# Attention of a hybrid decoder layer: units of four heads of a key group instead of two

## The chip, the cores and the metric

The kernel runs on one core of a Trainium2 chip. The core has five engines with an instruction queue each: TensorE (PE) for matrix products, VectorE (DVE), ScalarE (ACT), GpSimd (POOL) and SyncE (SP), which here only issues transfers. Matrix products land in PSUM, eight banks of 512 float32 columns on 128 partitions; everything else works from SBUF. An engine works its queue in order. The metric is the device time of one execution in microseconds (us).

## What is computed

One layer of a decoder on 1024 tokens of width 1024, all in float32. After a normalization and one input projection, eight attention heads (two key groups of four heads, head width 64) and eight groups of a gated spatial mixer run side by side; their outputs are joined, projected, normalized and added; then comes a SwiGLU feed-forward part. The change touches the attention alone. Every head has three branches, mixed by gates:

```python
o_c = softmax(q kc + bias) vc          # 63 compressed blocks
o_s = softmax(q ks + bias) vs          # selected blocks: all 16 are selected, so plain causal attention
o_w = softmax(q kw + bias) vw          # sliding window of 512 tokens
o = gb[..., 0:1] * o_c + gb[..., 1:2] * o_s + gb[..., 2:3] * o_w   # gb = sigmoid(gate logits)
```

The four heads of a group share their keys and values.

## The kernel before

Precision is kept by splitting each operand into a high part, rounded to the format that PE reads fast, and a low part, the rest. `split` (L165) makes both: the high part by a copy (ACT, L167), the low part by a subtraction (DVE, L173). `mm3` (L182) multiplies two split operands by three matmuls.

The attention loop (L640) goes over eight tiles of 128 query tokens, from tile 7, with most keys, to tile 0. In a tile it goes over the two key groups and over two pairs of heads in each: a unit is (tile, group, pair), 32 in all. A unit does the following.

- `load_q` (L568), two units ahead: two transfers from the scratch tensor `q_scr` on SP's queue into `qr`, and a split by POOL into `qt` (three buffers).
- For each head: logits by two matmuls for each chunk of columns (L674, L675) into one of two banks `ps_a`; DVE adds the position bias and keeps a running minimum (`biased`, L679; `plain`, L683) and writes them to a probability buffer `L`, one for each head, out of a ring of six; ACT takes the exponential of the three branches and their sums (L722).
- Three small instructions on DVE make the weights of the branches, gate divided by sum (L725 to L728), and POOL scales the probabilities by them (L733).
- Value products: a block is 128 keys. For two blocks PE transposes the scaled probabilities of both heads (L745) into a bank `ps_t` of 512 columns, out of three; `split` makes `ph` and `pl`; then each block takes two matmuls of 256 columns (L752, L754), which add up in the one bank `ps_p` over all blocks of the unit. The values hold high and low parts in 64 columns each, so that ACT copies the lower half of the result (`otmp`, L756) and DVE adds it to the upper half (`os`, L759); a last split makes `mixh` and `mixl`.

`output_proj` of the tile before (48 matmuls in the banks `ps_w`, two loads on POOL's queue, `xt` and the store of `h1` on SP's) stands ahead of the second of the four units of a tile, `pre_ffn` (eight transposes, two stores) ahead of the fourth. `with tc.high_priority(n)` moves what stands in it ahead by a number of places; a planner fixes each engine's order of instructions from that before the run, and the chip only waits on semaphores.

In SBUF, pools are laid on two stacks, and a pool that takes the place of an earlier one waits for the last user of it. On the left stack the attention's pools lie over the transposed input, first `pt`, `mix` and `late`, then `L` (its six pools taken from the top down), `o` and `q`. The feed-forward stage, written over the same room, starts when they come free. The value and gate projections `v_proj` (L482) run just ahead of the attention, tokens 4 to 7 of the input in the order 4, 5, 6, 7 and then 0 to 3, their banks taken in turn from `ps_w`, `ps_p` and `ps_t`.

## Time and profile before

| what | value |
|---|---|
| median of three runs | 1249.96 us (1245.37 to 1250.56) |
| profiled execution | 1250.03 us |
| its span, first to last instruction | 1248.3 us |
| mean granted clock of PE over the span | 0.993 of full speed |
| attention on DVE, first logit scan to last output split | 247.9 to about 595 us |

The profile is that of one execution. Busy time of an engine counts the time in which at least one of its instructions is under way; matmuls overlap each other in it, since the next starts while the one before still drains. PEld is the loading of weights into PE. A line such as L745 is one of the kernel's file; operations of a helper carry the helper's line.

### The profile page before, as it was taken

What the parts mean: (1) busy time and instruction counts of PE and PEld (TensorE: products, weight loads), DVE (VectorE), ACT (ScalarE), POOL (GpSimd) and SP (SyncE); (2) the same over time, 40 slices, a digit from 0 to 9 for tenths busy, and PEclk for the clock granted to TensorE, in tenths of its full rate; (3) what the DMA queues carried; (4) which work ended last, traced back from release to release, by engine and by line L of the source; (5) the groups of instructions that cost most, each with busy time, mean ns of one, the idle gap of its engine ahead of it and who ended that gap; (6) DMA issues with size and microseconds to landing.
All of it is one profiled execution on the core that took longest, in us unless ns stands there. A gap on an engine that the chain in (4) does not pass through costs nothing.

```text
span 1248.3 us, 18189 instructions
## 1 busy us (share of the span) xinstructions
PE 1201.0 (96%) x6074; PEld 1008.8 (81%) x6074; DVE 922.4 (74%) x2071; ACT 568.4 (46%) x1254; POOL 383.4 (31%) x454
## 2 busy tenths in 40 slices
PE   6999999889999999998899999999999999999997
PEld 5888878878888888887687888888888888888886
DVE  5646237668898988986599887876787647588996
ACT  4423022246777878886544332333332324444452
POOL 3315113155445446562051222201222101132341
PEclk9999999999999999999999999999999999999999
DMA  7212453321021121424414233223233189332235
GB/s 259 86 66 87 135 178 117 106 93 48 10 81 43 48 81 48 140 77 137 145 65 152 100 120 127 94 89 108 91 127 124 53 287 359 122 110 85 94 119 202
DMA packets 106229, 143.86 MB, mean 115 GB/s; under 512 B 8120, under 2 KB 64792, under 8 KB 106136
## 3 DMA queue, kind: packets, MB, share of 16 engines
q1 hardware_dynamic: 99552, 133.43, 32.4%
q0 software_dynamic: 2304, 4.20, 1.2%
q10 hardware_dynamic: 4280, 5.08, 1.2%
q8 instruction: 48, 0.79, 0.3%
q14 instruction: 45, 0.37, 0.1%
HBM read 103.60 MB, written 40.71 MB: 116 GB/s over the span
## 4 chain that ended last, share of the span: by engine, by line
PE 84%; DVE 9%; ACT 2%; issue 2%; DMA 1%; POOL 1%; SPq 0%; DVEq 0%; POOLq 0%; ACTq 0%
PE fb L185 16%; PE fb L183 15%; PE fb L184 15%; PE ps_w L183 4%; PE ps_w L184 4%; PE ps_w L185 4%; PE ps_a L183 4%; PE ps_a L184 3%; PE ps_a L185 3%; PE ps_t L745 3%; PE ps_p L754 2%; PE ps_p L752 2%; PE ps_a L674 2%; PE ps_a L675 2%; DVE pl L173 1%
## 5 line engine op out<-in xcount | busy, mean ns | idle before, releaser
L967 DVE TENSOR_TENSOR cc<-fb,cc 128x512 f32<-128x512 f32 x140 | 94.2, 685 | 55.9 <-PE fb L185 55.1
L722 ACT ACTIVATE L<-L,mm 128x64 f32<-128x64 f32 (+8 forms) x192 | 116.2, 608 | 37.0 <-DVE mm L679 36.2
L733 POOL TENSOR_SCALAR L<-L,wts 128x64 f32<-128x64 f32 (+8 forms) x192 | 108.4, 588 | 74.1 <-DVE wts L728 53.4
L848 POOL TENSOR_TENSOR cc<-sil 128x512 f32<-128x512 f32 x22 | 35.2, 1601 | 287.4 <-issue 226.3
L173 DVE TENSOR_TENSOR pl<-ps_t,ph 128x512 fp32r<-128x512 f32 (+1 forms) x160 | 101.6, 643 | 11.2 <-ACT ph L167 10.6
L167 ACT CAST op<-s 128x512 fp32r<-128x512 f32 x80 | 49.4, 620 | 121.5 <-PE fb L185 106.7
L184 PE MATMUL fb<-wdo,hido 128*128 128x512 f32 x264 | 102.7, 389 | 0.0
L183 PE MATMUL fb<-wdo,hido 128*128 128x512 f32 x264 | 101.9, 389 | 0.0
L185 PE MATMUL fb<-wdo,hido 128*128 128x512 f32 x264 | 100.4, 389 | 0.0
L184 PE MATMUL fb<-b_b,op 128*128 128x512 f32 x256 | 99.6, 389 | 0.0
L183 PE MATMUL fb<-b_b,op 128*128 128x512 f32 x256 | 99.3, 389 | 0.0
L185 PE MATMUL fb<-b_b,op 128*128 128x512 f32 x256 | 99.3, 389 | 0.0
L167 ACT CAST ph<-ps_t 128x512 fp32r<-128x512 f32 (+1 forms) x160 | 84.4, 555 | 25.6 <-PE ps_t L745 23.1
L745 PE MATMUL ps_t<-ident,L 128*128 128x128 f32 x592 | 88.6, 274 | 1.5 <-DVE pl L173 0.9
L674 PE MATMUL ps_a<-kt,qt 128*128 128x448 f32 (+4 forms) x208 | 74.7, 363 | 7.3 <-DVE L L683 2.8
L173 DVE TENSOR_TENSOR hido<-hidr,hido 128x512 fp32r<-128x512 f32 x77 | 60.8, 801 | 27.3 <-ACT hido L167 27.2
L167 ACT CAST hido<-hidr 128x512 fp32r<-128x512 f32 x77 | 47.4, 619 | 66.3 <-PE fb L185 22.8
L1046 POOL TENSOR_TENSOR tt<-wdr 128x512 f32<-128x512 f32 x22 | 36.1, 1644 | 134.5 <-DVE wdo L173 80.1
L754 PE MATMUL ps_p<-pl,vt 128*128 128x256 f32 x264 | 74.3, 303 | 3.1 <-DVE pl L173 3.0
L745 PEld LDWEIGHTS ps_t<-ident,L 128*128 128x128 f32 x592 | 68.9, 141 | 9.5 <-POOL L L733 1.8
L167 ACT CAST op<-wraw 128x512 fp32r<-128x512 f32 x60 | 37.1, 622 | 84.3 <-PE fb L185 75.6
L173 DVE TENSOR_TENSOR op<-s,op 128x512 fp32r<-128x512 f32 x80 | 63.9, 804 | 14.6 <-ACT op L167 13.8
(359 smaller groups left out, 3468.2 us busy)
## 6 DMA issues: line engine op xcount, KB each, us to landing
wraw<-in_w_gate_up_dram SPq DMA_DIRECT2D x40, 512.0 KB, 3.6
hidr<-hid_scr SPq DMA_DIRECT2D x77, 256.0 KB, 2.7
hid_scr<-sil SPq DMA_DIRECT2D x44, 256.0 KB, 2.0
wdr<-in_w_down_dram SPq DMA_DIRECT2D x44, 256.0 KB, 5.5
hid_scr<-cc SPq DMA_DIRECT2D x33, 256.0 KB, 2.0
xt<-in_x_dram SPq DMA_DIRECT2D x16, 512.0 KB, 3.6
raw<-in_w_in_dram SPq DMA_DIRECT2D x16, 512.0 KB, 4.3
gm_scr<-gmt SPq DMA_DIRECT2D x16, 256.0 KB, 2.6
```

The source lines that it names most:

```text
L167: nc.scalar.copy(hi, src)
L173: e.tensor_tensor(lo, src, fl(hi), op=ALU.subtract)
L183: nc.tensor.matmul(ps, sh, mh, start=first, stop=False)
L184: nc.tensor.matmul(ps, sh, ml, start=False, stop=False)
L185: nc.tensor.matmul(ps, sl, mh, start=False, stop=last)
L674: nc.tensor.matmul(ps[:, :w], qt[:, 0, hh, :], kt_[g][:, c0:c0 + w], start=True, stop=False)
L722: nc.scalar.activation(L[:, c0:c1], L[:, c0:c1], AF.Exp, bias=mm[:, col:col + 1], scale=-1.0, accum_out=sums[:, hh, br:br + 1])
L733: nc.gpsimd.tensor_scalar(pts[hh][:, c0:c1], pts[hh][:, c0:c1], wts[:, hh, br:br + 1], 1.0, op0=ALU.mult, op1=ALU.mult)
L745: nc.tensor.transpose(ps[:, (bi * 2 + hh) * P:(bi * 2 + hh + 1) * P], pts[hh][:, c0:c0 + P], ident)
L754: nc.tensor.matmul(pv[:, :256], v, pl[:, bi * 256:(bi + 1) * 256], start=False, stop=last)
L967: nc.vector.tensor_tensor(dst, ps, y_, op=ALU.add)
L1046: eng.tensor_tensor(dst, x_, y_, op=op)
```

## The change

A unit becomes (tile, group, first head, number of heads): four heads at once, two units for a tile, except that group 0 of the first tile stays in two units of two heads. That makes 17 units instead of 32.

- A group of value products is one block of four heads, and each product has 512 columns. One `ph` and `pl` hold one block instead of two.
- The ring `L` has eight buffers instead of six and lies last on the stack, above `o` and `q`. In tiles 2 to 0 two heads share a buffer and only the first four pools of the ring are used (`l_tile`).
- `load_q` loads four heads, one unit ahead, with one `qr` and two `qt` buffers.
- `gates` keeps 1 + exp(-x), without the reciprocal; the weights are 1 / (max(sum, 1e-30) * gates), by one combined instruction and one reciprocal.
- `output_proj` of the tile before stands ahead of the tile's last unit, `pre_ffn` between that unit's scaling and its value products. The priority numbers differ.
- `otmp` and `os` hold four heads, so that two sums of 64 x 256 and one split of 128 x 256 end a unit.

```diff
@@ gate
         nc.vector.tensor_scalar(gv_, gv_, 1.0, None, op0=ALU.add)
-        nc.vector.reciprocal(gv_, gv_)
@@ pools
-    for nm in ("pt", "mix", "late", "L", "o", "q"):
+    for nm in ("pt", "mix", "late", "o", "q", "L"):
         if nm == "L":
-            at[nm] = Ring("at_L", 6, "left")
-            at[nm].pools.reverse()
+            at[nm] = Ring("at_L", 8, "left")
...
+    def load_q(i, g, r0, nr):
+        qr = at["q"].tile([P, R, P], F32, name="qr", bufs=1)
+        h0 = g * R + r0
         for dup in range(2):
+            nc.sync.dma_start(out=qr[64 * dup:64 * dup + 64, :nr],
+                              in_=q_scr[h0:h0 + nr, :, i * P:(i + 1) * P].rearrange("h d t -> d h t"))
+        qt = at["q"].tile([P, 2, R, P], F32R, name="qt", bufs=2)
+        split(qt[:, 0, :nr], qt[:, 1, :nr], qr[:, :nr], "pool", "pool")
         return qt
...
-    order = [(i, g, pr) for i in TILES for g in range(G) for pr in range(2)]
+    order = [(7, 0, 0, 2), (7, 0, 2, 2), (7, 1, 0, 4)]
+    order += [(i, g, 0, 4) for i in TILES[1:] for g in range(G)]
+    QAHEAD = 1
...
+    packed = {}
+
+    def l_tile(i, n):
+        w = 64 + P * (i + 1) + P * min(i + 1, 5)
+        if i >= 3:
+            return at["L"].tile([P, 64 + S + 640], F32, "L")
+        if n % 2 == 0:
+            turn_ = packed["turn"] = packed.get("turn", -1) + 1
+            packed["t"] = at["L"].pools[turn_ % 4][1].tile([P, 64 + S + 640], F32, name="L")
+            return packed["t"][:, :w]
+        return packed["t"][:, 864:864 + w]
...
-    HP0, HP, HP2, HO, HF, HQ, HS, HV = 400, 100, 150, 100, 400, 300, 600, 200
+    HP0, HP, HP2, HO, HF, HQ, HS, HV = 400, 200, 250, 150, 500, 500, 900, 300
...
+        for un, unit in enumerate(units_):
+            _, g, r0, nr = unit
+            lastu = un == len(units_) - 1
+            if lastu and ti > 0:
+                with tc.high_priority(HO):
+                    pend = output_proj(TILES[ti - 1])
...
-                wts = small.tile([P, 2, 3], F32, name="wts")
-                nc.vector.tensor_scalar(wts, sums, 1e-30, None, op0=ALU.max)
-                nc.vector.reciprocal(wts, wts)
-                nc.vector.tensor_tensor(wts, wts, gates[...], op=ALU.mult)
+            nc.vector.scalar_tensor_tensor(wts[:, :nr], sums[:, :nr], 1e-30, gates[...], op0=ALU.max, op1=ALU.mult)
+            nc.vector.reciprocal(wts[:, :nr], wts[:, :nr])
...
+            if lastu and ti > 0:
+                with tc.high_priority(HF):
+                    pre_ffn(TILES[ti - 1], *pend)
             with tc.high_priority(HV):
...
-                    groups = [blocks[b:b + 2] for b in range(0, len(blocks), 2)]
+                n_ = nr * P
+                per = 512 // n_
+                groups = [blocks[b:b + per] for b in range(0, len(blocks), per)]
...
-                            nc.tensor.matmul(pv[:, :256], v, ph[:, bi * 256:(bi + 1) * 256], ...)
-                            nc.tensor.matmul(pv[:, :256], v, pl[:, bi * 256:(bi + 1) * 256], ...)
+                        nc.tensor.matmul(pv[:, :n_], v, ph[:, bi * n_:(bi + 1) * n_], ...)
+                        nc.tensor.matmul(pv[:, :n_], v, pl[:, bi * n_:(bi + 1) * n_], ...)
...
-                    tmp = at["o"].tile([64, 256], F32, name="otmp", bufs=OB)
+                tmp = at["o"].tile([64, 512], F32, name="otmp", bufs=OB)
```

## Rows read from the trace of the kernel before

**Rows 1.** The page's first part: busy us of each engine, share, instructions.
```profile
PE 1201.0 (96%) x6074; PEld 1008.8 (81%) x6074; DVE 922.4 (74%) x2071; ACT 568.4 (46%) x1254; POOL 383.4 (31%) x454
```

**Rows 2.** Windows: stretch and length, then busy us (instructions) by engine, granted clock.
```profile
core 0: us, PE busy (x) PEld busy (x) DVE busy (x) ACT busy (x) POOL busy (x), PEclk, DMA share, GB/s
250.00:300.00 50.00, 44.69 (x270) 38.82 (x270) 35.80 (x133) 27.92 (x64) 28.25 (x33) 0.93 0.27 85
300.00:550.00 250.00, 241.64 (x1584) 212.13 (x1583) 218.60 (x866) 194.29 (x520) 123.46 (x214) 1.00 0.21 64
550.00:600.00 50.00, 42.55 (x236) 35.43 (x235) 37.69 (x128) 35.34 (x106) 16.08 (x38) 0.96 0.47 148
```

**Rows 3.** PE's timeline (start, duration), a window of the feed-forward stage, one transpose.
```profile
359.99 0.28 PE L754 MATMUL ps_p<-pl,vt 128*128 128x256 f32 x1
...
360.34 0.28 PE L752 MATMUL ps_p<-ph,vt 128*128 128x256 f32 x1
360.46 0.60 PE L745 MATMUL ps_t<-ident,L 128*128 128x128 f32 x4
...
750.00:800.00 50.00, 50.00 (x222) 41.41 (x221) 37.34 (x54) 15.01 (x25) 6.50 (x4) 1.00 0.31 107
...
L745 PE MATMUL ps_t<-ident,L 128*128 128x128 f32 x592 | 88.6, 274 | 1.5 <-DVE pl L173 0.9 <-POOL L L733 0.2
```

**Rows 4.** Windows 300 to 550 for tiles ps_t, ps_p, ps_w; line L674 by width.
```profile
300.00:550.00 250.00, 78.83 (x526) 60.95 (x527) 90.24 (x142) 68.25 (x129) 1.00 0.21 64
...
300.00:550.00 250.00, 85.91 (x482) 68.70 (x482) 12.85 (x46) 8.51 (x23) 1.00 0.21 64
...
300.00:550.00 250.00, 70.32 (x258) 45.53 (x258) 0.00 (x0) 12.02 (x30) 1.00 0.21 64
...
L674 PE MATMUL ps_a<-kt,qt x159: 274/366/500, 299.7 to 549.5; 128*128 128x256 f32 x54, 128*128 128x384 f32 x41, 128*128 128x448 f32 x32, 128*128 128x512 f32 x16
```

**Rows 5.** Waits, 300 to 550 us: total us, times, longest.
```profile
DVE L L679 <- PE ps_t L745: 1.9, 1, 1.9
```

**Rows 6.** DVE's groups from 245 to 600 us: busy us, mean ns, idle before.
```profile
L173 DVE TENSOR_TENSOR pl<-ps_t,ph 128x512 fp32r<-128x512 f32 x136 | 92.0, 683 | 10.5 <-ACT ph L167 9.8
...
L759 DVE TENSOR_TENSOR os<-ps_p,otmp 64x128 f32<-64x128 f32 x64 | 17.9, 280 | 3.6 <-ACT otmp L756 2.9
...
L173 DVE TENSOR_TENSOR mixl<-os,mixh 128x128 fp32r<-128x128 f32 x32 | 12.0, 374 | 1.6 <-ACT mixh L167 1.6
...
L173 DVE TENSOR_TENSOR pl<-ps_t,ph 128x256 fp32r<-128x256 f32 x24 | 10.0, 416 | 0.8 <-ACT ph L167 0.8
...
L725 DVE TENSOR_SCALAR wts<-sums 128x6 f32<-128x6 f32 x32 | 8.1, 253 | 3.0 <-ACT L L722 2.7
...
L726 DVE RECIPROCAL wts<-wts 128x6 f32<-128x6 f32 x32 | 6.0, 187 | 0.4
L728 DVE TENSOR_TENSOR wts<-wts,gates 128x6 f32<-128x6 f32 x32 | 5.3, 166 | 0.3
...
L517 DVE RECIPROCAL gates<-gates 128x96 f32<-128x96 f32 x2 | 1.5, 730 | 0.0
```

**Rows 7.** Timeline from 570.7 to 572.8 us, the hand-over of the bank ps_p.
```profile
570.74 0.37 ACT L756 COPY otmp<-ps_p 64x256 f32<-64x256 f32 x1
...
572.71 0.55 PE L752 MATMUL ps_p<-ph,vch 128*128 128x256 f32 x1 [1.29 <-DVE os L759]
```

**Rows 8.** POOL's groups from 245 to 600 us: busy us, mean ns.
```profile
L733 POOL TENSOR_SCALAR L<-L,wts 128x640 f32<-128x640 f32 x40 | 31.6, 807 | 0.0
...
L733 POOL TENSOR_SCALAR L<-L,wts 128x64 f32<-128x64 f32 x64 | 19.7, 322 | 74.1 <-DVE wts L728 53.4 <-ACT L L722 10.8 <-ACT ph L167 5.4
```

**Rows 9.** By tile and line: ns min/median/max, first and last start in us.
```profile
L572 SPq DMA_DIRECT2D qr<-q_scr x64: 573/599/1487, 236.2 to 541.2; - x64
...
L489 ACT CAST vt<-ps_p x3: 352/372/373, 249.8 to 261.7; 128x256 fp32r<-128x256 f32 x3
...
L679 DVE CUSTOM_DVE_ANT_0 L<-ps_a,C x64: 207/224/227, 247.9 to 571.6; 128x64 f32<-128x64 f32 x64
```

More of the change, by code (lines that the diff above doesn't have):

```diff
@@ L137, in trunk_kernel @@
     gates = const.tile([P, NT, 24], F32, name="gates")
-    lead = const.tile([P, 112], F32, name="lead")
+    lead = const.tile([P, 48], F32, name="lead")
     nc.gpsimd.memset(lead[:, 0:1], 0.0)
@@ L566, in load_bc @@
         bcast_load(bc["post"], norm_mix_post[0])
-    def load_q(i, g, pr):
-        qr = at["q"].tile([P, 2, P], F32, name="qr", bufs=2)
-        h0 = g * R + 2 * pr
+    def load_q(i, g, r0, nr):
+        qr = at["q"].tile([P, R, P], F32, name="qr", bufs=1)
+        h0 = g * R + r0
         for dup in range(2):
-            nc.sync.dma_start(out=qr[64 * dup:64 * dup + 64],
-                              in_=q_scr[h0:h0 + 2, :, i * P:(i + 1) * P].rearrange("h d t -> d h t"))
-        qt = at["q"].tile([P, 2, 2, P], F32R, name="qt", bufs=3)
-        split(qt[:, 0], qt[:, 1], qr, "pool", "pool")
+            nc.sync.dma_start(out=qr[64 * dup:64 * dup + 64, :nr],
+                              in_=q_scr[h0:h0 + nr, :, i * P:(i + 1) * P].rearrange("h d t -> d h t"))
+        qt = at["q"].tile([P, 2, R, P], F32R, name="qt", bufs=2)
+        split(qt[:, 0, :nr], qt[:, 1, :nr], qr[:, :nr], "pool", "pool")
         return qt
     TILES = [7, 6, 5, 4, 3, 2, 1, 0]
-    order = [(i, g, pr) for i in TILES for g in range(G) for pr in range(2)]
+    order = [(7, 0, 0, 2), (7, 0, 2, 2), (7, 1, 0, 4)]
+    order += [(i, g, 0, 4) for i in TILES[1:] for g in range(G)]
+    QAHEAD = 1
     qts = {}
-    for key in order[:2]:
+    for key in order[:QAHEAD]:
         qts[key] = load_q(*key)
+    packed = {}
[8 more added lines that the diff above has]
+        return packed["t"][:, 864:864 + w]
     def load_wo(n):
@@ L589, in trunk_kernel @@
     wout_args = {}
-    HP0, HP, HP2, HO, HF, HQ, HS, HV = 400, 100, 150, 100, 400, 300, 600, 200
+    HP0, HP, HP2, HO, HF, HQ, HS, HV = 400, 200, 250, 150, 500, 500, 900, 300
     PVB, OPB, OB = "p", "w", 1
-    OPJ = (0, 1)
     WO0, WO1, WON, WOE = 1, 5, 2, nc.gpsimd
-    PRE = (1, 1)
     def output_proj(i):
```

212 lines of the change are left out of this document (105 added, 107 removed).

## The prediction

> **What bounds the kernel now.** I read the page's head first: TensorE (PE) is busy 1201.0 of 1248.3 us, VectorE (DVE) 922.4 [rows 1]. Matmuls overlap in that count, so it says little about slack. The windows view is better: from 550 to 600 us and from 250 to 300 us PE is busy for 42.6 and 44.7 of 50 us, with a granted clock below full speed on average (0.96 and 0.93) and DVE at 37.7 and 35.8; between them, from 300 to 550 us, DVE is busy 218.6 of 250 us (87%), ScalarE (ACT) 194.3 and GpSimd (POOL) 123.5 [rows 2]. These 350 us are the attention, the only stage that the change rewrites.
>
> What PE really issues there I work out from start-to-start times. Value products of 256 columns start 0.12 us apart (359.99 to 360.46 is 0.47 for four); the feed-forward stage, whose matmuls all have 512 columns and follow each other without a gap, runs 222 in 50 us, 0.225 each; four transposes span 0.60 us, less the 0.27 that one lasts that is three steps of 0.11 [rows 3]. From 300 to 550 us PE has 526 transposes, 482 value products, 258 output-projection matmuls and 318 logit matmuls, two for each of the 159 that one row lists by width (54 of 256 columns, 41 of 384, 32 of 448, 16 of 512, the other 16 of 320) [rows 4]. With 0.147, 0.173 and 0.20 for 320, 384 and 448 columns, read on the line between 0.12 and 0.225: 526 x 0.11 = 57.9, 482 x 0.12 = 57.8, 258 x 0.225 = 58.1, logits 2 x (6.5 + 7.1 + 6.4 + 3.6 + 2.4) = 52.0; together 225.8 of 250 us. So PE issues 90% of the stretch and DVE works 87%: neither alone is the bound, and about 24 us are lost there where one or the other is late. In the view of waits none of PE's or DVE's own is large; DVE's for a probability buffer that transposes still held came to 1.9 us, once [rows 5].
>
> **The change part by part.**
>
> *Value products of 512 columns.* By the loops there are 74 key blocks over the eight tiles (14, 13, 12, 11, 9, 7, 5, 3), so today 74 x 4 units x 2 = 592 products. They become 268 of 512 columns and, for the two starting units of two heads, 56 of 256: 536 go, 268 come. Two cost 0.235 to 0.24, one wide one 0.225 [rows 3]: 0.010 to 0.015 us saved each, 2.7 to 4.0 us in all; I take 3.2. The transposes stay 592, the logits 416.
> The Trainium skill's page "TensorE: Matmul & The Clock Gate", section "Back-to-back issue gap", gives a gap of N/2.4 + 2.5 ns; by that a pair saves only 2.5 ns and the whole edit 0.7 us, an estimate. The steps of [rows 3] are longer than the page's at both widths, and the measured ones decide; by either, the wide product in itself is worth little.
>
> *DVE.* Splits of transposed probabilities: 24 half-filled ones of 256 columns go (0.416 each), 12 full ones come (0.683): 10.0 - 8.2 = 1.8 us. Weights: three small instructions for 32 units, 8.1 + 6.0 + 5.3 = 19.4 us, become two for 17 units; at 0.17 and 0.22 (the reciprocal over 6 and over 96 elements, 187 and 730 ns, gives 6 ns an element, so 12 elements 223 ns) 6.6 us: 12.8 saved. The two gate reciprocals go: 1.5. The sums of value products: 64 of 128 columns, 17.9 us, become 30 of 256 columns and 4 as before; at the 256-column split's 0.416, 13.6: 4.3. Low halves of the mixer output: 32 x 0.374 = 12.0 become 15 x 0.416 + 2 x 0.374 = 7.0: 5.0. Together 25.4 of the 292.1 us that DVE is busy from 250 to 600 us [rows 2, 6].
> What that is worth has two bounds: nothing, if PE never waits for DVE, and 25.4 us, if each microsecond of it shows. Since DVE at 87% and PE at 90% are nearly level [rows 2, 4], and neither row nor wait names a sole bound, I take half: 12.7. The PE term I count alike, half of 3.2: 1.6. ACT loses instructions too (otmp, mixh, half-filled casts), counted at nothing: it is idle for 56 of the 250 us [rows 2].
>
> *Hand-over of the value bank.* There is one bank; between units it waits for ACT's copy and two DVE sums: before 572.7 us PE stood 1.29 us for them [rows 7]. Today 32 hand-overs of about 0.37 + 2 x 0.28 = 0.93 us; then 17 of about 0.68 (bounded by the 512-column split) + 2 x 0.416 = 1.5. 30 us of latency become 26; most of it is covered by transposes and logits. Worth 0 to 4 us; I take 1.
>
> *Units of four heads, eight buffers.* Scaling starts only when all four heads are exponentiated, and the first transposes want four heads scaled in two branches: 4 x 0.32 + 4 x 0.81 = 4.5 us of POOL in a middle tile against 2.3 today [rows 8]. Units halve, so the sum of this latency is unchanged; but a unit's four buffers come free only with its last transpose, and only one other unit can be on its way, where today two can. The cover is the value products of the unit before and the logits of the next. Bounds: 0, and all 4.5 us on some 15 units, 68 us. Nearest row: buffers were waited for once [rows 5], so I stay near zero: 0.2 us for each of 15, 3 us lost.
> The Trainium skill's page "Perfetto Trace Analysis", section "Optimization Strategy", says that evenly repeated gaps can mean too few buffers for the next tile. By that rule two more buffers should close gaps; [rows 5] puts 1.9 us on buffers, so I credit nothing.
>
> *Memory order and start.* The q tiles and first probability buffers move down the left stack: 40 KB of pt, mix and late, 3 of o, then 10 of q and the buffers, over 64 KB of transposed input; so they lie on its second half, which projections of token tiles 4 to 7 read. Today q lies above it and SP issues the first q load at 236.2 us [rows 9]. The bank order of the projections (w, p, t in turn) makes tile 5 the first that leaves bank p, with its cast at 249.8 us. After the change q cannot be loaded before that projection is done. Today's first logit scan on DVE is at 247.9. If tile 5 is still done at 249.5, then load, split and first logits follow no faster than today; today the first scan on DVE comes 11.7 us after the first q load, much of it spent behind projections, so the delay is at least nothing and at most 13.3 us (249.5 - 236.2). What hides it is the projections, which then have PE for themselves and are done sooner, tile 5 among them; without that cover the whole delay shows. I take 3 of 0 to 13.3, near the lower end, because the same projections stand in PE's way today. Behind the waiting q load on SP's queue stand only later q loads and the output weights; the second unit's q load waits besides for the single qr buffer.
> The loads of the feed-forward operand raw1, today into free space, must wait until tile 3 frees its upper buffers, three tiles before the operand is used: nothing.
>
> *output_proj and pre_ffn* move to the second of two units, from the second and fourth of four: the same 48 matmuls, 8 transposes, DVE passes, SP loads and stores and two POOL loads. On POOL the gate loads and rstd now stand behind the scaling of four heads, up to 4.5 us instead of 2.3; who waits is the next tile's output projection and the h2 stores, with half a tile before anyone needs them, so nothing, except after tile 0, where no scaling is left.
>
> **Sum.** - 12.7 - 1.6 - 1 + 3 + 3 = - 9.3 us. The profiled execution took 1250.0 us, the median of the three runs 1249.96: 1240.7, say 1241. Faster by over 0.5% means below 1243.7, the least a measurement of this kernel tells from no change.
>
> **Rivals.** (A) Forecast, 1232 to 1243.7, chance 0.40. (B) No measurable change: the DVE relief fills idle time because PE and the order of its queue set the pace; 3 us gained, start and end eat them: 1244 to 1256, say 1248. For it: PE at 90%. Against: DVE's 87% beside it. Chance 0.24. (C) Slower: the buffer ring. A unit lives from its first logits to its last transpose; when two units of four share eight buffers, the next logits stand behind the last transposes, and scaling (4.5 us of POOL plus about 1 us of exponentials) comes bare at each unit's end. Without the 3 us of that kind the sum is 1237.7, so from (1250.0 - 1237.7) / 15 = 0.8 us bare on each of 15 units the gain is gone; at 2 us the time is 1237.7 + 30 = 1268. For it: run-ahead falls from two units to one. Against: [rows 5], and that two more heads fit. Chance 0.22, from 1256 to 1275. (D) More: every microsecond taken from DVE and PE shows and the hand-overs count in full; with 25.4, 3.2 and 4 against the 6 us of cost the time is 1250.0 - 32.6 + 6 = 1223. For it: the 24 us lost [rows 4] are of that size. Against: it would need one engine to be late always. Chance 0.14, from 1215 to 1232.
>
> Below 1224 I leave a third of D and above 1264 a good third of C: 1224 to 1264. Within the forecast's own case, 1232 to 1243.7. Faster 0.40 + 0.14 = 0.54, same 0.24, slower 0.22.
>
> **What would show it.** The window of today's 300 to 550 us should be shorter with DVE busy about 19 us less there (25.4 x 218.6 / 292.1) and its share lower; 268 value products of 512 columns about 0.225 apart; the weights in 17 pairs of 0.39 us; the first logit scan a few microseconds later than 247.9; feed-forward unchanged in length, merely earlier. The prediction is wrong if DVE or PE wait for POOL's scaling or for transposes that hold a buffer for over 15 us in sum, if the first unit starts over 6 us late, or if the DVE time goes and the stretch keeps its length.

## The result, and the profile after

The changed kernel takes 1262.97 us, the median of four runs (1259.25 to 1265.23), beside 1249.35 for the kernel before on the same chip: a ratio of 1.0112, 95% interval 1.0076 to 1.0147. It is slower by some 13 us, where 9 us of gain were forecast. The profiled execution, on which the rows of the changed kernel rest, is the fastest of the four: 1259.25 us, span 1257.5. Against the span before, 1248.3, it shows 9.2 of the 13 us. The other three executions were 2.2 to 6.0 us longer, at a lower mean granted clock of PE (1 is full speed): 0.989, 0.988 and 0.985 against 0.993 here, while the executions of the kernel before that ran beside the experiments lie between 0.989 and 0.997. So a part of the 13 us, up to about 4 (the median less the profiled time), goes with a lower clock; where in the kernel it fell in those three, no trace shows.

The page's first part of the changed kernel answers to [rows 1]:

```profile
PE 1198.7 (95%) x5806; PEld 989.1 (79%) x5806; DVE 908.7 (72%) x1948; ACT 566.7 (45%) x1214; POOL 375.9 (30%) x424
```

268 matmuls and 123 DVE instructions are gone, as counted. The windows of the changed kernel answer to [rows 2] and to the feed-forward row of [rows 3]:

```profile
250.00:300.00 50.00, 41.28 (x253) 36.20 (x252) 30.07 (x119) 25.04 (x60) 27.16 (x30) 0.93 0.32 95
300.00:550.00 250.00, 234.94 (x1313) 190.47 (x1313) 206.07 (x752) 187.72 (x464) 119.76 (x188) 1.00 0.21 64
550.00:600.00 50.00, 46.10 (x242) 37.54 (x241) 32.62 (x119) 34.84 (x112) 18.18 (x44) 0.97 0.27 80
...
750.00:800.00 50.00, 50.00 (x222) 41.39 (x221) 37.29 (x53) 16.86 (x28) 6.50 (x4) 1.00 0.23 80
```

From 300 to 550 us DVE works 12.5 us less than before, and PE does not work more for it: its idle time grows from 8.4 to 15.1 us. The two kernels are not at the same point of their work in this window; a comparison between equal points follows the next table. The feed-forward stage runs at its old pace, 222 products in 50 us.

Where the time goes shows best in the last `otmp` copy of each tile, read off the timeline of each kernel (start, us; the rows with an e are experiments that come below, each one profiled execution):

| kernel | tile 7 | 6 | 5 | 4 | 3 | 2 | 1 | 0 | first feed-forward product (`fb`) |
|---|---|---|---|---|---|---|---|---|---|
| before | 325 | 374 | 425 | 471 | 511 | 544 | 571 | 593 | 624.7 |
| changed | 332 | 385 | 432 | 479 | 517 | 552 | 580 | 603 | 634.1 |
| e3: changed, all units of two heads | 323 | 376 | 424 | 468 | 508 | 543 | 569 | 589 | 620.7 |
| e6: changed, two heads in tiles 1 and 0 | 329 | 381 | 431 | 481 | 518 | 554 | 583 | 604 | 632.9 |
| e9: changed, weights by pairs | 335 | 383 | 431 | 479 | 517 | 549 | 576 | 597 | 629.0 |
| e17: changed, only the loads by four heads | 329 | 376 | 426 | 473 | 513 | 550 | 577 | 597 | 627.6 |

From the end of tile 6 to the end of tile 1 both kernels need nearly the same, 195.4 us after and 196.4 before. The loss against the kernel before lies ahead of that: 6.4 us at the end of tile 7, 10.4 at the end of tile 6, and still 9.4 at the end of tile 1 and 10.3 at the end of tile 0. Between the ends of tiles 6 and 1, where the work is the same, DVE is busy 14.2 us less, and PE idles 11.1 us instead of 6.5 (windows of the kernel before, then of the changed one):

```profile
374.00:571.00 197.00, 190.51 (x1247) 167.97 (x1246) 170.91 (x693) 157.10 (x447) 103.91 (x192) 1.00 0.25 77
```
```profile
385.00:580.00 195.00, 183.90 (x1040) 152.00 (x1040) 156.71 (x574) 150.24 (x404) 92.62 (x162) 1.00 0.25 76
```

PE's groups from 245 to 620 us (busy us, mean ns, then idle time just before them and what ended it) say which waits grew. The changed kernel, then the kernel before, whose transposes stand in [rows 3] with 1.5 us idle:

```profile
L758 PE MATMUL ps_t<-ident,L 128*128 128x128 f32 x592 | 90.8, 276 | 7.4 <-POOL L L741 6.9 <-DVE h2s L646 0.5
L682 PE MATMUL ps_a<-kt,qt 128*128 128x448 f32 (+4 forms) x208 | 76.8, 372 | 14.3 <-DVE mm L687 7.1 <-DVE L L691 5.5 <-DVE wts L734 1.1
...
L183 PE MATMUL ps_w<-whi,mixh 128*128 128x512 f32 x64 | 26.4, 412 | 4.7 <-DVE mixh L169 4.0 <-ACT mixh L167 0.7
```
```profile
L674 PE MATMUL ps_a<-kt,qt 128*128 128x384 f32 (+4 forms) x206 | 74.2, 363 | 7.3 <-DVE L L683 2.8 <-DVE mm L679 1.1 <-DVE wts L728 0.9
...
L183 PE MATMUL ps_w<-whi,mixh 128*128 128x512 f32 x64 | 26.7, 418 | 2.3 <-DVE mixh L169 2.0
```

Three waits grow: the logits' for a bank that DVE must empty (14.3 - 7.3 = 7.0 us), the transposes' for POOL's scaling (5.9), the output projection's for the mixer output (2.4): 15.3 us together. Two of the three sit at an end of the loop, as PE's timeline of the changed kernel shows:

```profile
276.78 0.90 PE L758 MATMUL ps_t<-ident,L 128*128 128x128 f32 x3 [6.70 <-POOL L L741]
```
```profile
601.03 0.50 PE L767 MATMUL ps_p<-pl,vt 128*128 128x512 f32 x1
605.49 0.50 PE L183 MATMUL ps_w<-whi,mixh 128*128 128x512 f32 x1 [3.95 <-DVE mixh L169]
```

The logits' wait has its clearest place in the first unit of four heads. Windows of 5 us from 301 to 321, value products alone (tile `ps_p`; the first number is PE's busy time, the count stands behind it), changed kernel:

```profile
301.00:306.00 5.00, 0.06 (x1) 0.00 (x0) 0.57 (x2) 0.37 (x1) 1.00 0.01 2
306.00:311.00 5.00, 0.00 (x0) 0.00 (x0) 0.00 (x0) 0.00 (x0) 1.00 0.18 52
311.00:316.00 5.00, 0.04 (x1) 0.07 (x1) 0.00 (x0) 0.00 (x0) 1.00 0.01 3
316.00:321.00 5.00, 2.97 (x9) 1.55 (x9) 0.00 (x0) 0.00 (x0) 1.00 0.01 2
```

For 15 us, from 300.78 to 315.96, no value product starts: those of the two heads before are used up, and the next four heads are not ready. PE has little but logits, which wait for DVE one after the other, and transposes in threes behind the scaling. POOL's timeline there:

```profile
305.59 0.62 POOL L171 TENSOR_SCALAR qt<-qr 128x512 fp32r<-128x512 f32 x1 [13.55 <-PE ps_a L683]
306.29 1.29 POOL L173 TENSOR_TENSOR qt<-qr,qt 128x512 fp32r<-128x512 f32 x1
308.98 8.65 POOL L741 TENSOR_SCALAR L<-L,wts 128x64 f32<-128x64 f32 x12 [1.40 <-DVE wts L737]
```

The costs of single instructions came as forecast: the weights in 17 pairs of 0.17 and 0.22 us (by tile: ns min/median/max), and wide products 0.23 us apart:

```profile
L734 DVE SCALAR_TENSOR_TENSOR wts<-sums,gates x17: 156/168/181, 264.7 to 583.0; 128x12 f32<-128x12 f32 x15, 128x6 f32<-128x6 f32 x2
L737 DVE RECIPROCAL wts<-wts x17: 184/224/228, 265.5 to 583.2; 128x12 f32<-128x12 f32 x15, 128x6 f32<-128x6 f32 x2
```
```profile
318.38 0.40 PE L767 MATMUL ps_p<-pl,vt 128*128 128x512 f32 x1
318.61 0.39 PE L765 MATMUL ps_p<-ph,vt 128*128 128x512 f32 x1
318.84 0.60 PE L758 MATMUL ps_t<-ident,L 128*128 128x128 f32 x4
```

To [rows 9] answer these starts: the first query load 12 us later than 236.2, the first logit scan 6 us later than 247.9, the first scaling at 275.0 against 269.7 (the last line is from the timeline of the kernel before).

```profile
L570 SPq DMA_DIRECT2D qr<-q_scr x6: 573/599/683, 248.5 to 257.8; - x6
...
L687 DVE CUSTOM_DVE_ANT_0 L<-ps_a,C x2: 215/218/220, 253.9 to 259.9; 128x64 f32<-128x64 f32 x2
...
L741 POOL TENSOR_SCALAR L<-L,wts x6: 317/800/1119, 275.0 to 278.6; 128x64 f32<-128x64 f32 x2, 128x1024 f32<-128x1024 f32 x2, 128x640 f32<-128x640 f32 x2
```
```profile
269.65 4.37 POOL L733 TENSOR_SCALAR L<-L,wts 128x64 f32<-128x64 f32 x6
```

### The profile page after: what moved, and what is told of

Read it like the earlier page. It is cut to its first block, busy times and chain, and to the rows that moved or that the text cites. A ratio compares the mean times of both kernels' runs of the same rounds, so it can differ in the third digit from the quotient of the medians.

```text
span 1257.5 us, 17294 instructions
## 1 busy us (share of the span) xinstructions
PE 1198.7 (95%) x5806; PEld 989.1 (79%) x5806; DVE 908.7 (72%) x1948; ACT 566.7 (45%) x1214; POOL 375.9 (30%) x424
## 4 chain that ended last, share of the span: by engine, by line
PE 84%; DVE 7%; DMA 3%; ACT 3%; issue 2%; POOL 1%; SPq 0%; DVEq 0%; POOLq 0%; ACTq 0%
PE fb L185 16%; PE fb L183 16%; PE fb L184 16%; PE ps_t L758 4%; PE ps_w L183 4%; PE ps_w L184 4%; PE ps_w L185 4%; PE ps_a L183 3%; PE ps_a L184 3%; PE ps_a L185 3%; PE ps_p L767 2%; PE ps_p L765 2%; PE ps_a L682 2%; PE ps_a L683 2%; DVE L L687 1%
## 5 line engine op out<-in xcount | busy, mean ns | idle before, releaser
L173 DVE TENSOR_TENSOR pl<-ps_t,ph 128x512 fp32r<-128x512 f32 x148 | 99.6, 686 | 14.8 <-ACT ph L167 14.0
L184 PE MATMUL fb<-wdo,hido 128*128 128x512 f32 x264 | 102.7, 389 | 0.0
L184 PE MATMUL fb<-b_b,op 128*128 128x512 f32 x256 | 99.6, 389 | 0.0
L167 ACT CAST ph<-ps_t 128x512 fp32r<-128x512 f32 x148 | 83.9, 586 | 24.7 <-PE ps_t L758 22.8
L758 PEld LDWEIGHTS ps_t<-ident,L 128*128 128x128 f32 x592 | 73.4, 142 | 21.8 <-POOL L L741 7.9
L682 PE MATMUL ps_a<-kt,qt 128*128 128x448 f32 (+4 forms) x208 | 76.8, 372 | 14.3 <-DVE mm L687 7.1
L1063 POOL TENSOR_TENSOR tt<-wdr 128x512 f32<-128x512 f32 x22 | 35.8, 1631 | 135.0 <-DVE wdo L173 79.9
L173 DVE TENSOR_TENSOR op<-s,op 128x512 fp32r<-128x512 f32 x80 | 63.6, 800 | 15.1 <-ACT op L167 14.2
L683 PE MATMUL ps_a<-kt,qt 128*128 128x448 f32 (+4 forms) x208 | 67.1, 326 | 0.0
```

Source lines behind the costliest of these rows:

```text
L167: nc.scalar.copy(hi, src)
L173: e.tensor_tensor(lo, src, fl(hi), op=ALU.subtract)
L184: nc.tensor.matmul(ps, sh, ml, start=False, stop=False)
L682: nc.tensor.matmul(ps[:, :w], qt[:, 0, hh, :], kt_[g][:, c0:c0 + w], start=True, stop=False)
L683: nc.tensor.matmul(ps[:, :w], qt[:, 1, hh, :], kt_[g][:, c0:c0 + w], start=False, stop=True)
L758: nc.tensor.transpose(ps[:, (bi * nr + hh) * P:(bi * nr + hh + 1) * P], pts[hh][:, c0:c0 + P], ident)
```

## The experiments

All medians; the ratio is that to the kernel before on the same chip, with its 95% interval. The kernel before had medians of 1249.15 to 1250.58 beside them. By these intervals, a difference of under some 3 us between two of the experiments is not clear of noise.

| run | us | ratio |
|---|---|---|
| changed kernel | 1262.97 | 1.0112 [1.0076, 1.0147] |
| e1, q on top of the stack | 1261.56 | 1.0100 [1.0081, 1.0120] |
| e2, output weights loaded later | 1262.27 | 1.0105 [1.0085, 1.0124] |
| e3, all units of two heads | 1247.05 | 0.9986 [0.9973, 1.0000] |
| e4, kernel before with inverse gates | 1244.31 | 0.9968 [0.9953, 0.9982] |
| e5, two heads in tiles 7 and 6 | 1255.07 | 1.0037 [1.0021, 1.0053] |
| e6, two heads in tiles 1 and 0 | 1257.86 | 1.0067 [1.0044, 1.0090] |
| e7, weights by pairs | 1265.18 | 1.0117 [1.0093, 1.0141] |
| e8, third logit bank | 1281.46 | 1.0254 [1.0229, 1.0279] |
| e9, weights by pairs, old addresses | 1254.20 | 1.0045 [1.0025, 1.0064] |
| e10, two heads at both ends | 1253.65 | 1.0027 [1.0016, 1.0038] |
| e11, kernel before moved by 32 bytes | 1260.91 | 1.0091 [1.0077, 1.0106] |
| e12, e4 with a ring of eight | 1242.93 | 0.9946 [0.9933, 0.9959] |
| e13, e9 with narrow products | 1254.26 | 1.0047 [1.0029, 1.0065] |
| e14, e3 with q on top | 1244.65 | 0.9967 [0.9954, 0.9980] |
| e15, e9 with q on top | 1253.71 | 1.0035 [1.0013, 1.0058] |
| e16, e13, projection at the last pair | 1253.94 | 1.0035 [1.0020, 1.0050] |
| e17, only the loads by four heads | 1253.88 | 1.0039 [1.0022, 1.0055] |

**The parts of the change by themselves: e1 to e4.** e1 puts q back on top of the stack, with the ring of eight under it and taken from the top:

```diff
-    for nm in ("pt", "mix", "late", "o", "q", "L"):
+    for nm in ("pt", "mix", "late", "L", "o", "q"):
...
+            at[nm].pools.reverse()
...
-            packed["t"] = at["L"].pools[turn_ % 4][1].tile(...)
+            packed["t"] = at["L"].pools[turn_ if turn_ < 4 else 4 + turn_ % 4][1].tile(...)
```


> The changed kernel with the q tiles and the first probability buffers back above the transposed input (stack order pt, mix, late, L, o, q; ring taken from the top). Theory S (the start costs the 7 us that tile 7 ends later, because q must wait for the projection of token tile 5): first q load near 236 us again instead of 248.5, first scaling before 272 us instead of 275.0, time 1250 to 1257. Rival U (the 7 us are the four-head unit's): first q load near 236 us, tile 7 still ends near 332 us, time 1260 to 1266.

The first query load came at 236.6 us and the first scaling at 267.3, 8 us earlier; tile 7 ended at 329, 3 us earlier, and the total is 1.4 us less, within the noise. The late start is not where most of the loss lies.

```diff
-    WO0, WO1, WON, WOE = 1, 5, 2, nc.gpsimd
+    WO0, WO1, WON, WOE = 2, 5, 2, nc.gpsimd
```


> The changed kernel with the last output weights loaded and split one unit later. Theory S2 (in the start the queue of POOL matters: weight splits and a four-head q split stand ahead of the first scaling, from 266.4 to 275.0 us): first scaling at 266 to 270 us, PE's wait of 6.9 us before the first transposes mostly gone, time 3 to 6 us under the changed kernel's 1263. Rival (only the late q load counts): first scaling earlier, but tile 7 ends within 1 us of 332 us and the time stays at 1261 to 1265.

In e2 the first scaling stayed at 275.0, so its premise was not met, and it tells nothing.

e3 is the changed kernel with every unit of two heads; memory order, eight buffers, priorities and inverse gates stay. `output_proj` and `pre_ffn` stay at the tile's last unit, which now has two heads (e16 tests that place):

```diff
-    order = [(7, 0, 0, 2), (7, 0, 2, 2), (7, 1, 0, 4)]
-    order += [(i, g, 0, 4) for i in TILES[1:] for g in range(G)]
+    order = [(i, g, r0, 2) for i in TILES for g in range(G) for r0 in (0, 2)]
```


> The changed kernel with units of two heads throughout, all else as changed (order of pools, eight buffers, one q unit ahead, inverse gates, priorities). Theory A (four-head units eat in the steady tiles what DVE gains): with units of two the stretch from the end of tile 7 to the end of tile 1 takes 235 to 242 us instead of 248, time 1250 to 1257. Rival (DVE work taken away is worth nothing here): that stretch stays at 245 to 250 us, time 1260 or more, since the start is as late.

1247.05: units of four heads cost 1262.97 - 1247.05 = 15.9 us, more than the whole loss. This is a net figure, for what four heads save on DVE and PE is gone from e3 too. In the profiled executions, which are 12.2 us apart, the changed kernel ends tile 7 8.6 us behind e3, tile 3 8.1 and tile 0 13.7: the loss arises in tile 7 (8.6 us) and in tiles 2 to 0 (5.6), while tiles 6 to 3 lose nothing. Of the three waits above the logits' falls below what it was before and the output projection's returns to its old size; the transposes' stays, as the start is still late (e3, PE's groups):

```profile
L757 PE MATMUL ps_t<-ident,L 128*128 128x128 f32 x592 | 90.8, 276 | 7.3 <-POOL L L740 5.8 <-DVE pl L173 1.0
L681 PE MATMUL ps_a<-kt,qt 128*128 128x448 f32 (+4 forms) x208 | 75.9, 369 | 4.7 <-DVE mm L686 2.6 <-DVE L L690 1.7
...
L183 PE MATMUL ps_w<-whi,mixh 128*128 128x512 f32 x64 | 25.6, 400 | 2.1 <-DVE mixh L169 2.0
```

e4 does one part alone, in the kernel before: the reciprocal of `gates` goes, and the weights are made by two instructions.

```diff
-        nc.vector.reciprocal(gv_, gv_)
...
-                nc.vector.tensor_scalar(wts, sums, 1e-30, None, op0=ALU.max)
-                nc.vector.reciprocal(wts, wts)
-                nc.vector.tensor_tensor(wts, wts, gates[...], op=ALU.mult)
+                nc.vector.scalar_tensor_tensor(wts, sums, 1e-30, gates[...], op0=ALU.max, op1=ALU.mult)
+                nc.vector.reciprocal(wts, wts)
```


> The kernel before with the inverse gates in the weights alone, about 7 us less of DVE (one small instruction of 32 units and two reciprocals less). Theory A and my prediction (half of what DVE loses shows): 1244 to 1247. Rival (worth nothing): 1248 to 1251, same within 0.3%.

It takes about 19.4 + 1.5 us off [rows 6] and puts 32 x (0.165 + 0.186) = 11.2 back, 9.7 us of DVE; the ratio gives 4.0 us of gain (2.2 to 5.9). That is 0.41 of what DVE lost, and the interval takes in the forecast's one half.

**Where four heads cost: e5, e6, e10.** These change the list `order` alone: units of two heads in tiles 7 and 6 (e5), in 1 and 0 (e6, where tile 7 begins with four heads as well), in 7, 6, 1 and 0 (e10). `TWO` stands for these tiles.

```diff
-    order = [(7, 0, 0, 2), (7, 0, 2, 2), (7, 1, 0, 4)]
-    order += [(i, g, 0, 4) for i in TILES[1:] for g in range(G)]
+    order = [(i, g, r0, 2 if i in TWO else 4) for i in TILES for g in range(G) for r0 in ((0, 2) if i in TWO else (0,))]
```


> The changed kernel with tiles 7 and 6 in units of two heads, tiles 5 to 0 in units of four. Its last otmp copy of tile 7 stood at 332 us in the changed kernel and at 323 with two-head units everywhere, and the distance stayed 8 to 11 us until tile 1. Theory S (the loss lies in the first four-head unit because it comes on top of the late loads and the weight splits on POOL): the loss of tile 7 goes and does not come back; tile 7 ends near 323, tile 5 near 424, tile 1 near 572, total about 1254. Rival M (any first four-head unit behind two-head units leaves the matrix engine without value products, since the two heads before it have too few of them to cover the logits and the scaling of four): tile 7 ends near 323, but the gap moves into tile 5 and its end is 432 or later, total 1259 to 1263.

The median, 1255.07, is near theory S; the gap in the trace is that of M. Value products of e5 by windows of 5 us, as above:

```profile
375.00:380.00 5.00, 2.42 (x15) 1.93 (x13) 0.56 (x2) 0.37 (x1) 1.00 0.00 0
380.00:385.00 5.00, 0.00 (x0) 0.00 (x0) 0.00 (x1) 0.00 (x0) 1.00 0.00 0
385.00:390.00 5.00, 0.00 (x0) 0.00 (x0) 0.00 (x0) 0.00 (x0) 1.00 0.19 56
390.00:395.00 5.00, 0.00 (x0) 0.00 (x0) 0.00 (x0) 0.00 (x0) 1.00 0.26 105
395.00:400.00 5.00, 2.75 (x8) 1.42 (x9) 0.00 (x0) 0.00 (x0) 1.00 0.29 69
```

A gap of the same kind, 17 us from 378.50 to 395.56, stands now in tile 5: it belongs to the change-over from two heads to four, wherever it lies. But it costs less here. Tile 5 ends at 430.5, 51.6 us behind tile 6 (46.8 in the changed kernel, 48.1 in e3): some 4 us lost, where tile 7 of the changed kernel lost 8.6. By the medians, two-head units in tiles 7 and 6 are worth 7.9 of the 15.9 us although the gap is still there; what makes it dearer in tile 7, no run tells apart. The profiled execution of e5, 1258.9 us, is the slowest of its eight, so that its total is not the one to compare.

> The changed kernel with tiles 1 and 0 in units of two heads, the others in units of four. Theory E (a four-head unit at the end costs some 5 to 6 us, as the distance of the two kernels grows from 8 to 14 us between the ends of tile 1 and tile 0): tile 1 ends near 580 as in the changed kernel, tile 0 near 597, first feed-forward product near 628, total about 1257. Rival (the loss at the end is that of the start carried on; the last tile only shows it): tile 0 near 603, total 1262.

1257.86, 5 us less, as theory E had it. But E's 5 to 6 us came from a misread row: tile 1 of e3 ends at 569, not 572, so the distance to the changed kernel grows by 2.5 us between the ends of tile 1 and tile 0, not by 6. And in the profiled execution tile 0 ended at 604, not 597, with the first feed-forward product at 632.9 against 634.1; its mean granted clock was 0.984, with the lower of PE's two levels (0.50) from 280 to 290 us. That the median agrees may be luck, the two intervals overlap, and a gain at the end is not shown.

> The changed kernel with tiles 7, 6, 1 and 0 in units of two heads and only tiles 5 to 2 in units of four. Two-head units in 7 and 6 alone took 8 us off, in 1 and 0 alone 5. Theory (the cost sits at the two ends of the loop, where the matrix engine has no value products to set beside four heads of logits, and adds): 1263 - 13 = 1250; tiles 5 to 2 take as long as with two-head units everywhere (167 us from the end of tile 6 to the end of tile 2), but the first four-head unit behind two-head units still shows a gap in tile 5. Rival (each change-over between unit sizes costs about the same, wherever it lies): 1255 or more.

1253.65: the two gains do not add up in full (9.3 us of 13). Tile 5 takes 51.6 us, 3.5 more than in e3, so a part of the gap has moved there again.

**The hand-over inside a unit: e7, e9, e8.** e7 and e9 make weights and scaling for two heads at a time; a unit is still four heads for the rest.

```diff
-            wts = small.tile([P, R, 3], F32, name="wts")
-            nc.vector.scalar_tensor_tensor(wts[:, :nr], sums[:, :nr], ...)
+            for hp in range(0, nr, 2):
...
+              wts = small.tile([P, 2, 3], F32, name="wts")
+              nc.vector.scalar_tensor_tensor(wts, sums[:, hp:hp + 2], ...)
```


> The changed kernel, with the weights and the scaling of a four-head unit made for two heads at a time, so that POOL scales the first two heads while the other two still have their logits: 17 more pairs of weight instructions of 0.39 us on the vector engine. Theory P (the hand-over at the end of a four-head unit is what costs: POOL's 8.65 us of scaling stand bare in the first one): the first value product of the first four-head unit comes 4 us earlier than 315.96, tile 7 ends near 328, and some 4 us are left off the total, 1258 to 1259; with a like gain at the end 1256. Rival L (the fill waits for the logits, their scans and exponentials of four heads, not for the scaling): within 2 us of 1263.

The attention ended earlier (first feed-forward product 630.6), yet the total was 1265.18. The windows of e7 and, under them, of e9 at the same place show why: 216 products in 50 us instead of 222, at full granted clock.

```profile
750.00:800.00 50.00, 50.00 (x216) 40.23 (x215) 35.77 (x51) 16.88 (x28) 6.50 (x4) 1.00 0.24 80
```
```profile
750.00:800.00 50.00, 50.00 (x222) 41.42 (x221) 36.41 (x52) 16.21 (x27) 6.50 (x4) 1.00 0.31 100
```

e9 differs from e7 in nothing but the size of the tile `wts`, four buffers of 48 bytes a partition instead of 24:

```diff
-              wts = small.tile([P, 2, 3], F32, name="wts")
+              wts = small.tile([P, R, 3], F32, name="wts")[:, :2]
```


> The kernel with weights by pairs again, the weight tile at its size in the changed kernel (48 bytes a partition, of which 24 are used), so that everything allocated behind it lies where it lies there. In the run before, the attention ended 3 to 4 us earlier than in the changed kernel (first feed-forward product 630.6 against 634.1 us), but the feed-forward products that read op took 0.232 us instead of 0.227 each, 11 us in all. Theory A (the 96 bytes by which op had moved make them slow): 0.227 again, total 1265.2 - 11 = 1254. Rival (the products are slow for another reason that came with the edit, such as the order of the queues): 1265 again.

1254.20, as theory A had it. So the hand-over of weights for four heads at once costs 1262.97 - 1254.20 = 8.8 us, over half of the 15.9. POOL now scales the first pair while the second has its logits, so that 4.36 us of scaling stand ahead of the first unit's products instead of 8.65. Yet the gap there is only 1.4 us shorter, 302.52 to 316.26 instead of 300.78 to 315.96, since the products still want the second pair, and tile 7 even ends 3 us later than in the changed kernel. The gain shows in tile 6 (47.8 us instead of 53.3) and in tiles 2 to 0 (79.9 instead of 86.5; 80.9 in e3). The rows are e9's second scaling, the two ends of its gap, and those of the changed kernel:

```profile
310.58 4.36 POOL L742 TENSOR_SCALAR L<-L,wts 128x64 f32<-128x64 f32 x6 [1.35 <-DVE wts L738]
```
```profile
302.52 0.28 PE L768 MATMUL ps_p<-pl,vt 128*128 128x256 f32 x1
...
316.26 0.40 PE L766 MATMUL ps_p<-ph,vch 128*128 128x512 f32 x1
```
```profile
300.78 0.28 PE L767 MATMUL ps_p<-pl,vt 128*128 128x256 f32 x1
...
315.96 0.47 PE L765 MATMUL ps_p<-ph,vch 128*128 128x512 f32 x1
```

e8 gives the logits a third bank and takes one from the transposes:

```diff
-    TAGS = {"a": 2, "t": 3, "p": 1, "w": 2}
+    TAGS = {"a": 3, "t": 2, "p": 1, "w": 2}
```


> The changed kernel with three banks ps_a for the logits and two ps_t for the transposes instead of two and three. Theory B (in a four-head unit the logits come one after another and the matrix engine waits for the vector engine to empty a bank, 31 waits of the vector engine on ps_a with 31 us and 7 of the matrix engine on it): a third bank takes half of it, about -5 us, 1258. Rival T (with two banks the transposes wait for the splits, whose eviction sets the pace of the value products): +10 us or more, 1273 or later.

1281.46, rival T. The logits' wait shrinks, but the value products, which had next to none, wait now for the splits, 5.8 us, a part of the 18.5 that the run lost (e8, PE's groups from 245 to 640 us):

```profile
L682 PE MATMUL ps_a<-kt,qt 128*128 128x448 f32 (+4 forms) x208 | 75.2, 368 | 9.1 <-DVE mm L687 7.5 <-DVE L L691 1.1
...
L767 PE MATMUL ps_p<-pl,vt 128*128 128x512 f32 (+1 forms) x145 | 60.9, 424 | 5.8 <-DVE pl L173 5.4
```

**What is left of four heads: e13, e16, e17.** e13 takes e9 and makes the products for two heads at a time, 256 columns, all of the first pair's ahead of the second's; e16 puts `output_proj` ahead of the last pair; e17 closes each pair (`otmp`, `os`, mixer output) and writes its products behind its own scaling, so that only the loads go by four heads: the queries', and those of the output weights, two for each of the second to fifth unit.

```diff
-                n_ = nr * P
+                n_ = 2 * P
...
-                for gi, grp in enumerate(groups):
+                for hp, gi, grp in [(hp, gi, grp) for hp in range(0, nr, 2) for gi, grp in enumerate(groups)]:
...
-                            nc.tensor.matmul(pv[:, :n_], v, ph[...], ...)
+                            nc.tensor.matmul(pv[:, hp * P:hp * P + 256], v, ph[...], ...)
```


> Weights by pairs as in the run with the same addresses (1254.2), and the value products of a four-head unit made for two heads at a time as well, 256 columns, two blocks to a group, the first pair's before the second's; loads, logits order and the closing sums stay with four heads. Theory W (wide products cost by their granularity: no product of a unit can start before all four heads are scaled): the 7 us to the two-head kernel go, 1247 to 1249, although there are 268 products more, at 0.23 for one wide against 0.237 for two narrow ones, +2 us. Rival (the width is neutral or a gain, the 7 us lie in the loads or closing sums of four heads): 1254 to 1257.

1254.26: the width of the products, together with their order by pairs, is worth nothing that can be measured, either way.

```diff
-            if lastu and ti > 0:
-                with tc.high_priority(HO):
-                    pend = output_proj(TILES[ti - 1])
...
+              if lastu and ti > 0 and hp == nr - 2:
+                with tc.high_priority(HO):
+                    pend = output_proj(TILES[ti - 1])
```


> Pairs and narrow products (1254.3), with the output projection of the tile before ahead of the last pair of heads of a tile instead of the last four. Theory J (its place makes a part of the 7 us, since the distance to two-head units grows from 4 to 7 us in tile 0): 1250 to 1252. Rival (place neutral): 1253 to 1256.

1253.94: the place is neutral too.

```diff
             for hp in range(0, nr, 2):
...
-            with tc.high_priority(HV):
+              with tc.high_priority(HV):
...
-                m0 = g * 2 + r0 // 2
+                  m0 = g * 2 + (r0 + hp) // 2
```


> As the run with the projection at the last pair, and the products, the otmp copy, the sums and the output split of each pair written behind its own scaling: a four-head unit is then only the query load. Theory K (the order of the program by four heads, all logits of a unit ahead of its products, makes what is left): 1247 to 1248, as two-head units. Rival Q (the query loads by four heads, one unit ahead, make it): 1252 to 1255.

1253.88, rival Q: what is left, 7 us, comes with the loads by four heads and one unit ahead. How is open. PE's waits for logits and transposes are not the whole of it, 6.5 and 9.4 us here against 4.7 and 7.3 in e3, and tile by tile the distance to e3 grows slowly, from 0 at the end of tile 6 to 7 us at the end of tile 0. e9, as far behind e3 in its median, has 6.9 us of distance at the end of tile 6 already. So the 7 us need not be the same thing in both, and that the loads make them is what is left over, not shown.

**The start, and a better kernel: e14, e15, e12.** e14 and e15 put q on top, with the edit of e1, in e3 and in e9.

> The changed kernel with two-head units everywhere (1247.05) and with q on top of the stack as before, the ring of eight below it, taken from the top. Theory (the 3 us to the inverse gates alone, 1244.3, are the memory order: first query load at 248 us instead of 236): 1243 to 1245, first scaling near 267 us. Rival (priorities and the place of the output projection make them): 1246 to 1248.

1244.65, 2.4 us less than e3 and level with the inverse gates alone.

> Weights by pairs at the same addresses (1254.2) with q on top of the stack. Theory (an earlier start is worth 3 us once the hand-over does not eat it; with the changed kernel's hand-over it was worth 1.4): 1251. Rival (the first four-head unit still stands bare, whenever the loop starts): 1253 to 1255.

1253.71, 0.5 us less than e9. In the profiled executions, though, e15 ends tile 7 11.4 us earlier than e9, tile 1 7.2 and tile 0 5.4 (591.9 against 597.3); 3.5 are left at the first feed-forward product, 0.7 in the total. So most of the earlier start is lost late, from the end of tile 1 on; why is open.

e12 is e4 with eight buffers in the ring:

```diff
-            at[nm] = Ring("at_L", 6, "left")
+            at[nm] = Ring("at_L", 8, "left")
```


> The kernel before with the inverse gates and with a ring of eight probability buffers instead of six, all else as before: two heads, stack order, priorities. The inverse gates alone gave 1244.3. Theory (two more buffers let the logits run a unit ahead of the scaling, and shorten the waits of the matrix engine on scaled probabilities): 1241 to 1243. Rival (the buffers are not what a two-head unit waits for): 1244 to 1245.

1242.93, the best of all, 0.5% faster than before (0.41 to 0.67%). PE's wait for logits falls to 3.7 us. The first query load stands at 168.7 us, since the larger ring moves q into other room, but the first scaling at 259.5 only; how much the buffers give and how much the room is not told apart, and against e4 the 1.4 us lie within the two intervals. That evenly repeated gaps can mean too few buffers, as the Trainium skill's page "Perfetto Trace Analysis" has it in "Optimization Strategy", is so neither borne out nor refuted here; in the changed kernel, with the same eight buffers, the gaps stayed.

```profile
L673 PE MATMUL ps_a<-kt,qt 128*128 128x384 f32 (+4 forms) x206 | 73.9, 361 | 3.7 <-DVE L L682 1.4 <-DVE mm L678 1.3 <-DVE wts L728 0.3
```

## Why the prediction was wrong

The step that failed is "Units of four heads, eight buffers": 3 us were taken, 15.9 measured (e3). The figures are not quite alike, for the 15.9 is net of what four heads save. The forecast credited 7.9 us to that (half of the 25.4 - 9.7 us of DVE that are not the inverse gates'), 1.6 and 1, so that its own net figure for this step was a gain of 7.5. The rest of the forecast, half of 9.7 for the inverse gates against 3 for the memory order, makes 1.9 us of gain, and e3 measured 1.8 by its ratio. So the whole miss, some 23 us, lies in this step.

It said that the sum of the latency is unchanged, because units halve as it doubles, and then spread a small bare rest evenly over 15 units. That agrees with the middle, where the next unit's logits lie beside the value products of four heads: from the end of tile 7 to that of tile 3 the changed kernel takes 185.0 us, e3 185.5. It is not true at the first unit of four heads, behind two heads, whose products do not cover it (15 us without value products in the changed kernel and, moved by two tiles, 17 in e5), nor in tiles 2 to 0 (86.5 us against 80.9). These two places were not looked at. That the last tiles lose because their units have only 7, 5 and 3 key blocks to cover the next unit is argued, not shown: e9 takes 79.9 us there, but e6, with two heads in two of the three, took 85.5.

By medians, the 15.9 us are 8.8 for weights and scaling of four heads at once (e9), none for the products (e13) or the place of the projection (e16), and 7 that are left when only the loads go by four heads (e17), whose way is not settled.

- *DVE.* The durations were right: weights 6.6 us as forecast, `os` 13.5 against 13.6. Half as the share that shows agrees with the inverse gates (4.0 of 9.7 us, e4). What the sums and splits that only four heads save are worth is not told apart: no run has them without the units, and 15.9 is the net of both. DVE's busy time on the page fell by 13.7 us, not 25.4, in part because short instructions overlap their neighbours and count once (e4: 9.7 us by durations, 922.4 - 915.2 = 7.2 on the page), in part because the low halves of the mixer output saved 2.7 instead of 5.0; the rest of the difference was not followed up.
- *Value products.* 0.23 apart as forecast, and the 1.6 us credited to the width is nil within what e13 and e9 can tell. The Trainium skill's page "TensorE: Matmul & The Clock Gate", section "Back-to-back issue gap", has the gap that the forecast drew on for a matmul by itself; by it the edit was worth 0.7 us, an estimate, which these runs cannot tell from nothing either.
- *Memory order and start.* 3 us taken; the first scan came 6.0 us late, and undoing the order gives 2.4 us with two heads (e14), 1.4 in the changed kernel (e1), neither clear of noise: the size agrees as far as this tells.
- *Hand-over of the value bank.* 1 us was credited; no run did it alone, and at the last tile the output projection waits for the sums behind it 2.4 us longer than before.

Of the rivals, C is nearest: its range holds the time, and it named the scaling that comes bare. But it put this on the buffer ring and on every unit's end. DVE's waits for a buffer that transposes hold stay small (1.0 us in all ahead of the logit scans), and the middle units lose nothing. Of the signs that were to show the forecast wrong, the last one appeared: DVE's time went, 14.2 us from the end of tile 6 to that of tile 1, and the stretch kept its length. The start, 6.0 us late, stood at the edge of another.

## What to carry to other kernels

Where a pipeline is made coarser, the middle may keep its pace while the ends pay (here tile 7, and tiles 2 to 0): for the first and the last units, and for each place where the size changes, set what the unit ahead still offers as cover against the whole latency of the new one. Pass results on in the smaller grain (here weights and scaling for two heads) even where the work is grouped in the larger. And undo the size alone while keeping the rest of a change: e3 and e4 told within two runs which part gave and which took.

## What was not expected of the hardware

The feed-forward products that read `op` slow down when it lies elsewhere by 96 bytes (e7 against the changed kernel) or by 32 (e11 against the kernel before), at full granted clock. e11 is the kernel before with one edit, a filler tile of 32 bytes less:

```diff
-    lead = const.tile([P, 112], F32, name="lead")
+    lead = const.tile([P, 104], F32, name="lead")
```


> The kernel before with nothing changed but the filler tile lead, 104 floats instead of 112, so that all that is allocated behind it moves by 32 bytes. Theory A (the matrix engine reads the moving operand op more slowly when it starts 32 bytes off): the 1776 feed-forward products that read op take 0.232 to 0.233 us instead of 0.227, +11 us, 1261; the attention, which ended no later in the run that showed this, as before. Rival: 1250, nothing in the addresses matters.

1260.91 us, 11 more than before. Its page, and that of e9 under it, show that the products of `op` last 395 ns instead of 389, while those of `hido` do not change; those that multiply the same `b_b` by another operand, `plain_op`, take 390 against 389 (L184), so `b_b` alone is not what slows them:

```profile
L183 PE MATMUL fb<-wdo,hido 128*128 128x512 f32 x264 | 101.9, 389 | 0.0
L184 PE MATMUL fb<-b_b,op 128*128 128x512 f32 x256 | 101.1, 395 | 0.0
```
```profile
L184 PE MATMUL fb<-b_b,op 128*128 128x512 f32 x256 | 99.6, 389 | 0.0
```

The start-to-start time goes from 50 / 222 = 0.225 to 50 / 216 = 0.231 us, 0.006 us on each of 1728 products (768 with `b_b`, 480 with `b_t`, 240 each with `b_b12t` and `b_r1t`), 11 us. The changed kernel does not suffer from it: its larger `sums` and `wts` add four buffers of 2 x 24 bytes, 192, and `lead` gives back 64 floats, 256, which moves what follows by 64 bytes. Which addresses are slow was not tried further; 32 bytes are, and so is e7's shift, 160 bytes less than the kernel before. The profiled executions of all other runs have 222 or 223 products in this window, so their differences do not come from this.
